# A DeltaNet recurrence that prepares its next tile early, and a merge whose pool is opened during the last attention

## The chip, the cores and the metric

The kernel runs on one core of a Trainium2 chip. Its metric is the device time of one execution in microseconds (us); smaller is better. The engines are named as the profile names them: PE does matrix products (PEld is its weight loading), DVE is the vector engine, ACT the scalar engine, POOL the GpSimd engine, SP the queue that issues most of the DMAs.

## The reference, cut to what matters

One layer of a streaming encoder for 1024 prompt rows and 64 sample rows. Four branches read one projection of the normalised input; their outputs are gated and summed, and a feed-forward block follows.

```python
def token_mixers(u, past, p, l):
    proj = u @ p['w_in'][l]
    fox, dif, sb, gdn, gates = jnp.split(proj, SPLITS, axis=-1)
    o_fox  = query_sweep(fox_core, ...)      # forgetting attention
    o_diff = query_sweep(diff_core, ...)     # two softmaxes a head: p1 - lam * p2
    o_sb   = query_sweep(sb_core, ...)       # stick-breaking attention
    o_g, s_new = gated_delta_chunked(gq, gk, gv, g, beta, s0, 64)
    gate = jax.nn.sigmoid(gates).reshape(B, T, 4, D_MODEL)
    merged = sum(gate[:, :, i] * (o.reshape(B, T, 256) @ wb[i]) for i, o in enumerate(branches))
    return merged @ p['w_out'][l], new_state

def gated_delta_chunked(q, k, v, g, beta, s0, chunk):
    # free of the state: sol = triangular_solve(m + I, [v*beta, k*beta*exp(gcum)]); u0, kcum = split(sol); qk
    def step(S, xs):                         # one after the other, 64 rows each
        v_new = u_i - kc_i @ S
        o = (q_i * exp(g_i)) @ S + a_i @ v_new
        S = S * exp(g_last) + (k_i * exp(g_last - g_i)).T @ v_new
        return S, o
```

The inputs keep these shapes; the feed-forward block, the norms and the short convolution are not touched by the change.

## The kernel before, in words

The work is cut into row tiles of 128 (tile 8 is the 64 sample rows). A tile framework records the instructions, gives each tile of memory a slot from its pool, orders the instructions of each engine ahead of time and writes the semaphores; on the chip each engine then takes its own list from the front. A pool's tag has a fixed number of slots (`bufs`). Products are done in float16 pairs, so most of them are three matmuls (high x high, high x low, low x high).

Stages in order of time: the projections and the DeltaNet's first pass; then three attentions, `attend_sb`, `attend_fox` and `attend_diff`, each over 2 head pairs and 9 query tiles; then the merge; then the output projection and the feed-forward block. Two lists of generators are worked off beside the attentions. `dense` holds PE-heavy work; from `attend_sb` on its main part is `spill_gates`: 16 units of 256 gate columns (4 a branch, in the order sb, fox, diff, gdn), each of 6 pieces, each piece 24 matmuls into one PSUM bank `pgs`, an ACT eviction `ths` and a POOL DMA to DRAM `gtd_sb`, `gtd_fox`, `gtd_diff`, `gtd_gdn`. `side` holds latency-bound work: during `attend_diff` it is `gdn_seq`, the recurrence. `fill(us)` is called once for each query tile (twice in `attend_diff`); it takes that much from `dense` and one step from `side`.

A gate unit's weights come through the tag `w32` of the pool `wp`: two DMA loads of 128x1024 into two of its **three** slots, each split into a float16 pair by ACT (`wh`) and DVE (`wl`, L64), after which the slot is free. The merge's branch weights use the same tag, under the name `wb32`, and are split into `wbh` and `wbl`.

`gdn_seq` opens the pool `gp3` on the right side of SBUF. For each of nine tiles it loads, makes the state-free part (`py`, `px`, the block-diagonal `ttbd`, `pu`, `pk`, `kc`), then takes one or two steps of 64 rows, each a chain `pks`, `vn`, `vh`, `pds`, `S32`, `Sh`/`Sl`. Its PSUM tiles come from the tag `g`, two banks. The result goes through `osg` to `od_gdn`.

Only when `attend_diff` and `gdn_seq` are recorded is `gp3` closed and the merge's pool `br` opened, also on the right side: it holds `oT` (a branch's output, read back from DRAM), `wbh`, `wbl`, and the first gate tiles `thg`. The merge takes the branches in the order sb, fox, diff, gdn, 24 pieces each: 6 matmuls into `ptb`, the gate's tanh on ACT, and DVE or POOL adds into `mg`.

In profile rows and rows of order the numbers at the ends of names are often left out or cut: `w` and `wb` are `w32` and `wb32`, `tt` and `t` are `tt32` and `t11`, `y` is `y21`, `u` is the normalised input for `pgs`, `rec1b` and `rec2b` are the records that the first pass left in DRAM.

Of the kernel before, what the change touches and what calls it, by code (L numbers as in the profile page):

```python
# [9 lines left out]
F16 = mybir.dt.float16  # L10
# [7 lines left out]
P = 128  # L18
D = 1024
# [34 lines left out]
def tile_hybrid_encoder(ctx, tc, i, o):  # L54
# [836 lines left out]

    def new_state(S32, Sh, Sl):
        acopy(Sh, S32, 16.0)
        stt(Sl, S32, 16.0, Sh, ALU.mult, ALU.subtract)

    def gdn_seq(g3):
# [20 lines left out]
        def fresh_state():  # L917
            return (g3.tile([P, NH, 64], F16, tag="Sh", name="Sh", bufs=2),
                    g3.tile([P, NH, 64], F16, tag="Sl", name="Sl", bufs=2))
# [4 lines left out]
        for hf in range(2):  # L924
            sync.dma_start(S32s[64 * hf:64 * hf + 64], i["state_gdn"][0, 0].rearrange("h d e -> d h e"))

        for t in [8] + list(range(8)):
            n = rows(t)
            nch = 1 if t == 8 else 2
            S32 = S32s if t == 8 else S32p  # L930
            if t in (8, 0):
                Sh, Sl = fresh_state()
                new_state(S32, Sh, Sl)
            t32 = t32s[t % 2]
            t11 = g3.tile([P, NH, 32], F32, tag="t11", name="t11", bufs=2)
            y21 = g3.tile([P, NH, 32], F32, tag="y21", name="y21", bufs=2)
# [2 lines left out]
            for c in range(nch):  # L939
                up, dn = slice(64 * c, 64 * c + 32), slice(64 * c + 32, 64 * c + 64)  # L940
                sync.dma_start(t32[up, :, 0:32], xv[2 * t + c, 0])
                sync.dma_start(t32[dn, :, 32:64], xv[2 * t + c, 1])
                sync.dma_start(t32[up, :, 32:64], nd[2 * t + c, :, 2].rearrange("h j i -> j h i"))
                sync.dma_start(t11[64 * c:64 * c + 32], xtv[2 * t + c])

            py = pgd("py")
            px = pgd("px")
            for c in range(nch):
                lo_, up_ = slice(64 * c, 64 * c + 32), slice(64 * c + 32, 64 * c + 64)
                for h in range(NH):  # L950
# [6 lines left out]
            for c in range(nch):  # L957
                sl = slice(64 * c, 64 * c + 64)
                acopy(bd[sl, 0, :, sl], t32[sl])
                tt(bd[sl, 1, :, sl], t32[sl], bd[sl, 0, :, sl], ALU.subtract)  # L960
            rec1 = g3.tile([P, 1536], F16, tag="rec1", name="rec1b", bufs=1)
            rec2 = g3.tile([P, 1536], F16, tag="rec2", name="rec2b", bufs=2)
            sync.dma_start(rec1[:n], r1d[t, 0:n])
            sync.dma_start(rec2[:n], r2d[t, 0:n])
            if n < P:
                vec.memset(rec2[n:], 0.0)
            qe = g3.tile([P, NH, P], F16, tag="qe", name="qe", bufs=2)
            sync.dma_start_transpose(out=qe[:, :, 0:n], in_=qed[t * P:t * P + n])
            kbe = rec1[:, 0:1024].rearrange("p (l h d) -> p l h d", l=2, h=NH)
            vb = rec1[:, 1024:].rearrange("p (l h e) -> p l h e", l=2, h=NH)  # L970
            kd = rec2[:, 0:1024].rearrange("p (l h d) -> p l h d", l=2, h=NH)
# [12 lines left out]
            pk4 = pk.rearrange("p (h i) -> p h i", h=NH)  # L984
            acopy(kc[:, :, :n], pk4[:, :, :n])
            tt(kc[64:128, :, :n], pk4[64:128, :, :n], kc[64:128, :, :n], ALU.subtract)

            zt = g3.tile([P, BW], F32, tag="zt", name="ztg", bufs=2)
            gps.dma_start(zt[:n], zd[t * P:t * P + n])
            z4g = zt.rearrange("p (h e) -> p h e", h=NH)  # L990

            po = pgd("pog")
            for c in range(nch):
                sl = slice(64 * c, 64 * c + 64)
                e4 = eg[:, c, t * NH:(t + 1) * NH]
                pks = pgd("pks")
                for h in range(NH):
                    pe.matmul(pks[sl, h * 64:h * 64 + 64], lhsT=kc[:, h, sl], rhs=Sh[:, h], start=True, stop=False)
                    pe.matmul(pks[sl, h * 64:h * 64 + 64], lhsT=kc[:, h, sl], rhs=Sl[:, h], start=False, stop=True)
                S1 = g3.tile([P, NH, 64], F32, tag="S1", name="S1", bufs=2)  # L1000
                tt(S1, S32, bc(e4[:, :, None], [P, NH, 64]), ALU.mult)
                vn = g3.tile([P, NH, 64], F32, tag="vn", name="vn", bufs=2)
                vh = vhs[c]
                stt(vn[sl].rearrange("p h e -> p (h e)"), pks[sl, 0:256], -(2.0 ** -5),
                    u0[sl].rearrange("p h e -> p (h e)"), ALU.mult, ALU.add)
                acopy(vh[sl, 0], vn[sl])
                tt(vh[sl, 1], vn[sl], vh[sl, 0], ALU.subtract)
                pds = pgd("pds")
                for h in range(NH):
                    for q, (a, b) in enumerate(((0, 0), (0, 1), (1, 0))):  # L1010
                        pe.matmul(pds[:, h * 64:h * 64 + 64], lhsT=kd[:, a, h], rhs=vh[:, b, h], start=(q == 0), stop=(q == 2))
                for h in range(NH):
                    dst = po[sl, h * 64:h * 64 + 64]
                    pe.matmul(dst, lhsT=qe[:, h, sl], rhs=Sh[:, h], start=True, stop=False)
                    pe.matmul(dst, lhsT=qe[:, h, sl], rhs=Sl[:, h], start=False, stop=False)
                    pe.matmul(dst, lhsT=aa[:, 0, h], rhs=vh[:, 0, h], start=False, stop=False)
                    pe.matmul(dst, lhsT=aa[:, 0, h], rhs=vh[:, 1, h], start=False, stop=False)
                    pe.matmul(dst, lhsT=aa[:, 1, h], rhs=vh[:, 0, h], start=False, stop=True)
                stt(S32.rearrange("p h e -> p (h e)"), pds[:, 0:256], 2.0 ** -9, S1.rearrange("p h e -> p (h e)"), ALU.mult, ALU.add)
                Sh, Sl = fresh_state()  # L1020
                if not (t == 8 or (t == 7 and c == 1)):
                    new_state(S32, Sh, Sl)
                yield 0.0
            if t == 8:
                gps.dma_start(o["s_gdn_state"][0, 0].rearrange("h d e -> d h e"), S32[0:64])
# [49 lines left out]
    with tc.issue_after(last_tanh[0].ins):  # L1075
        pre = act.preload_act_table_set("natural_log_exp_and_others")
    wide[0] = False
    with tc.issue_after(pre.ins):
        dense += [spill_gates(b, sp, d2) for b in gtd for d2 in range(4)]
        attend_sb()  # L1080
    drain(dense, proj[1])
    drain(dense, dense[0])
# [6 lines left out]
    drain(side)  # L1089
    cb_.close()  # L1090
    pj_.close()
    gd_ = ExitStack()
    g3 = gd_.enter_context(tc.tile_pool(name="gp3", bufs=1, side="right", reuse_waits="tile"))
    side.append(gdn_seq(g3))
    attend_diff()
    drain(side)
    gd_.close()
    br_ = ExitStack()
    brp = br_.enter_context(tc.tile_pool(name="br", bufs=1, side="right", reuse_waits="tile"))
    drain(dense)  # L1100
    ap_.close()
    gp_ = ExitStack()
# [12 lines left out]

    gt_pool = gp_.enter_context(tc.tile_pool(name="gates", bufs=1, reuse_waits="tile"))

    wbr = i["w_branch"][0]
    pbk = (psc, pgd, psc, pgd, psc)
    nb_ = [0]  # L1120
    mg = [(brp if d < 3 else gt_pool).tile([P, T], F32, tag=f"mg{d}", name=f"mg{d}") for d in range(KD)]
    order = ("sb", "fox", "diff", "gdn")
    for bi, b in enumerate(order):
        j = bidx[b]
        oT = brp.tile([P, 2, 2, T], F16, tag="oT", name="oT", bufs=2)
        if b in ("sb", "fox"):
            for pr in range(2):
                gps.dma_start(oT[:, :, pr], od[b][pr])
        else:
            sync.dma_start_transpose(out=oT.rearrange("p l r t -> p (l r) t"), in_=od[b])  # L1130
        wbh = brp.tile([P, 2, D], F16, tag="wbh", name="wbh", bufs=2)
        wbl = brp.tile([P, 2, D], F16, tag="wbl", name="wbl", bufs=2)
        for k in range(2):
            w32 = wp.tile([P, 4, BW], F32, tag="w32", name="wb32", bufs=3)
            wv = w32.rearrange("p a b -> p (a b)")[:, :D]
            sync.dma_start(wv, wbr[j, k * P:(k + 1) * P])
            acopy(wbh[:, k], wv, WS)
            stt(wbl[:, k], wv, WS, wbh[:, k], ALU.mult, ALU.subtract)
        last = bi == len(order) - 1
        for c in {1: (1, 2), 2: (3, 0)}.get(bi, ()):  # L1140
            load_out(c)
        for d, (off, n) in [(d, PIECES[p]) for p in (0, 2, 1) for d in range(KD)] if last else \
                [(d, p) for d in range(KD) for p in PIECES]:
            th = (brp if bi == 0 else gt_pool).tile([P, 364], F32, tag=("th0" if bi == 0 else "th"), name="thg",
                                                    bufs=(4 if bi == 0 else 12))
            sync.dma_start(th[:, :n], gtd[b][d * P:(d + 1) * P, off:off + n])
            act.activation(th[:, :n], th[:, :n], AF.Tanh)
            pt = pbk[nb_[0] % len(pbk)]("ptb")
            nb_[0] += 1
            last_ptb = gemm_a(pt, (wbh, wbl), d * P, oT[:, 0], oT[:, 1], off, n, 2)  # L1150
            if bi == 0:
                stt(mg[d][:, off:off + n], th[:, :n], 1.0, pt[:, :n], ALU.add, ALU.mult)
            else:
                stt(th[:, :n], th[:, :n], 1.0, pt[:, :n], ALU.add, ALU.mult)
                tt(mg[d][:, off:off + n], mg[d][:, off:off + n], th[:, :n], ALU.add,
                   eng=vec if (d % 3 == 2 if last else off >= 728) else gps)
            if last:
                sl = slice(off, off + n)
                acopy(mT[:, 0, d, sl], mg[d][:, sl], 0.5 * IWS)
                stt(mT[:, 1, d, sl], mg[d][:, sl], 0.5 * IWS, mT[:, 0, d, sl], ALU.mult, ALU.subtract)  # L1160
# [351 lines left out]
```

## Time and profile before

| | |
|---|---|
| time, median of 3 runs | 1853.46 us (1852.04 to 1858.17) |
| the profiled execution | 1856.4 us, of which the span of the trace is 1854.7 us |
| PE busy | 1740.3 us, 94% of the span, 14364 matmuls |
| DVE busy | 1251.0 us, 67% |
| ACT busy | 866.6 us, 47% |
| POOL busy | 307.1 us, 17% |

The busy share is a mean over stages with different limits, and a matmul's length is modelled, so the table says only where to look. Places in time are given in us from the start of the span.

### The profile page before, as it was taken

The page shows a single profiled execution, that of the slowest core. Times are in us where ns is not written, and L with a number is a line of the kernel's source. Part 1 is how long each engine was busy: PE and PEld are TensorE (multiplying, and loading weights), DVE is VectorE, ACT ScalarE, POOL GpSimd, SP SyncE. Part 2 cuts the span into 40 slices and gives each one's busy share as a digit, 9 for nine tenths or more (in the row PEclk, how much of TensorE's full clock was granted, in tenths as well). Part 3 has the DMA queues.
Part 4 walks back from the last instruction along what each step waited for, and adds up shares of the span by engine and source line. Part 5 has one row for each costly group of instructions (what it writes and reads, how often), then busy time and mean ns, then how long its engine had stood idle before and what let it go on. Part 6 is the DMA issues. An engine that isn't in the chain of part 4 may idle for free.

```text
span 1854.7 us, 36819 instructions
## 1 busy us (share of the span) xinstructions
PE 1740.3 (94%) x14364; PEld 1236.0 (67%) x14364; DVE 1251.0 (67%) x2589; ACT 866.6 (47%) x1819; POOL 307.1 (17%) x478
## 2 busy tenths in 40 slices
PE   7999898999999899999758999999999999999998
PEld 5678775655776566666534578777758668577573
DVE  7659872877788567877847886757637456465465
ACT  6336553998666345655544533423314223133132
POOL 2104342121110212332313630000000000000002
PEclk9999999999999999999759999999999999999999
DMA  7287689888899875755548746412211113012113
GB/s 226 49 100 205 207 241 229 181 156 183 186 242 213 180 177 126 172 143 142 118 152 282 223 138 106 102 52 69 69 35 58 46 46 92 25 45 69 35 47 102
DMA packets 412767, 244.29 MB, mean 132 GB/s; under 512 B 266278, under 2 KB 390450, under 8 KB 412456
## 3 DMA queue, kind: packets, MB, share of 16 engines
q1 hardware_dynamic: 398944, 205.67, 46.0%
q0 software_dynamic: 13648, 36.27, 6.7%
q8 instruction: 112, 1.84, 0.4%
q14 instruction: 63, 0.52, 0.1%
HBM read 123.39 MB, written 60.53 MB: 99 GB/s over the span
## 4 chain that ended last, share of the span: by engine, by line
PE 58%; DVE 6%; DMA 6%; ACT 2%; issue 1%; POOL 0%; SPq 0%; DVEq 0%; POOLq 0%; ACTq 0%
PE po L1434 12%; PE pgs L183 4%; PE pgs L185 4%; PE pgs L184 4%; DMA pt<-st 3%; PE pb L1317 3%; PE pb L1318 3%; PE pb L1319 3%; PE pa L1319 2%; PE pc L1318 2%; PE pa L1318 2%; PE pa L1317 2%; PE pc L1319 2%; PE pc L1317 2%; PE pout L165 1%
## 5 line engine op out<-in xcount | busy, mean ns | idle before, releaser
L183 PE MATMUL pgs<-u,wh 128*128 128x364 f16 (+1 forms) x768 | 246.2, 321 | 6.0 <-ACT ths L61 5.9
L185 PE MATMUL pgs<-u,wl 128*128 128x364 f16 (+1 forms) x768 | 246.2, 321 | 0.0
L184 PE MATMUL pgs<-u,wh 128*128 128x364 f16 (+1 forms) x768 | 246.1, 320 | 0.0
L1434 PE MATMUL po<-wh,hT 128*128 128x512 f16 (+1 forms) x792 | 238.2, 380 | 0.6 <-DVE x2a L64 0.6
L1434 PEld LDWEIGHTS <-hT 128*128 128x128 f16 (+1 forms) x1188 | 109.2, 99 | 120.0 <-issue 7.6
L64 DVE SCALAR_TENSOR_TENSOR x2a<-po,x2a 128x512 f32<-128x512 f32 x108 | 74.4, 689 | 141.5 <-PE po L1434 141.3
L61 ACT ACTIVATE wh<-w32f 128x1024 f16<-128x1024 f32 (+1 forms) x90 | 80.3, 926 | 160.7 <-PE po L1434 111.6
L1317 PE MATMUL pb<-X,wh 128*128 128x288 f16 (+1 forms) x528 | 147.5, 280 | 2.4 <-DMA X<-nsh 2.1
L64 DVE SCALAR_TENSOR_TENSOR wl<-w32f,wh 128x1024 f16<-128x1024 f32 (+1 forms) x90 | 94.6, 1065 | 80.0 <-ACT wh L61 79.9
L1318 PE MATMUL pb<-X,wh 128*128 128x288 f16 (+1 forms) x528 | 147.8, 280 | 0.0
L1319 PE MATMUL pb<-X,wl 128*128 128x256 f16 (+1 forms) x528 | 146.9, 280 | 0.0
L1434 PE MATMUL po<-wl,hT 128*128 128x512 f16 (+1 forms) x396 | 142.1, 379 | 0.0
L1317 PEld LDWEIGHTS <-wh 128*128 128x128 f16 x1232 | 120.8, 98 | 31.3 <-issue 2.3
L1318 PEld LDWEIGHTS <-wh 128*128 128x128 f16 x1232 | 120.8, 98 | 30.4 <-issue 2.4
L1319 PEld LDWEIGHTS <-wl 128*128 128x128 f16 x1232 | 120.8, 98 | 27.0 <-issue 0.4
L184 PEld LDWEIGHTS <-wh 128*128 128x128 f16 x912 | 89.8, 98 | 56.6 <-issue 8.5
L165 PE MATMUL pd<-wh,u 128*128 128x256 f16 (+1 forms) x448 | 123.8, 276 | 1.3 <-ACT e L61 1.3
L183 PEld LDWEIGHTS <-wh 128*128 128x128 f16 x912 | 89.9, 99 | 52.3 <-issue 2.7
L167 PE MATMUL pd<-wh,u 128*128 128x256 f16 (+1 forms) x448 | 123.7, 276 | 0.0
L185 PEld LDWEIGHTS <-wl 128*128 128x128 f16 x912 | 89.9, 99 | 50.6 <-issue 1.4
L166 PE MATMUL pd<-wl,u 128*128 128x256 f16 (+1 forms) x448 | 123.5, 276 | 0.0
L71 POOL TENSOR_SCALAR fss<-fss 128x1 f32<-128x1 f32 (+1 forms) x9 | 2.0, 219 | 661.6 <-ACT fsq L1463 661.6
(393 smaller groups left out, 4662.6 us busy)
## 6 DMA issues: line engine op xcount, KB each, us to landing
w<-in_w_in_dram SPq DMA_DIRECT2D x56, 512.0 KB, 5.3
w32f<-in_w_ffn_gate_dram SPq DMA_DIRECT2D x20, 512.0 KB, 5.0
w32f<-in_w_ffn_up_dram SPq DMA_DIRECT2D x20, 512.0 KB, 3.9
w32f<-in_w_ffn_down_dram SPq DMA_DIRECT2D x20, 512.0 KB, 3.8
xt<-in_x_prompt_dram SPq DMA_DIRECT2D x8, 512.0 KB, 6.6
wb<-in_w_branch_dram SPq DMA_DIRECT2D x8, 512.0 KB, 5.8
w<-in_w_out_dram SPq DMA_DIRECT2D x8, 512.0 KB, 3.7
x2a<-in_x_prompt_dram SPq DMA_DIRECT2D x8, 512.0 KB, 7.2
```

The source lines that it names most:

```text
L61: return act.activation(out, in_, AF.Copy, scale=scale)
L64: return vec.scalar_tensor_tensor(out=out, in0=in0, scalar=s, in1=in1, op0=op0, op1=op1)
L165: pe.matmul(ps[:n, :N], lhsT=a, rhs=wh[:, k, :N], start=(k == 0), stop=False)
L166: pe.matmul(ps[:n, :N], lhsT=a, rhs=wl[:, k, :N], start=False, stop=False)
L167: pe.matmul(ps[:n, :N], lhsT=b, rhs=wh[:, k, :N], start=False, stop=(k == K - 1))
L183: pe.matmul(ps[:, :n], lhsT=a, rhs=xh[:, k, off:off + n], start=(k == 0), stop=False)
L184: pe.matmul(ps[:, :n], lhsT=a, rhs=xl[:, k, off:off + n], start=False, stop=False)
L185: mm = pe.matmul(ps[:, :n], lhsT=b, rhs=xh[:, k, off:off + n], start=False, stop=(k == K - 1))
L1317: pe.matmul(ps[:, :n], lhsT=wh[:, k], rhs=xh_, start=(start and k == 0), stop=False, skip_group_check=not start)
L1318: pe.matmul(ps[:, :n], lhsT=wh[:, k], rhs=xl_, start=False, stop=False, skip_group_check=not start)
L1319: mm = pe.matmul(ps[:, :n], lhsT=wl[:, k], rhs=xh_, start=False, stop=(k == 3), skip_group_check=not start)
L1434: pe.matmul(ps[h * n:h * n + n], lhsT=hts[k + h][:, a, tk:tk + n], rhs=w[:, k + h], start=(k == 0 and a == 0 and w is wh), stop=(k + nh >= ...
```

## The change

Three edits. In `gdn_seq` the tile's work is cut into `load` and `prepare`; the next tile's `load` stands ahead of a tile's steps and its `prepare` between the two steps. `px` becomes a part of `py`'s bank and `pks` a part of `po`'s, so that a two-step tile takes 6 banks in turn where it took 9. In the main sequence 16 us of gate units are taken ahead of `attend_sb`, and the gate generators no longer stand under the order edge of the table load. And a generator `open_merge` follows `gdn_seq` on `side`: it closes `gp3`, opens `br`, and records the loads of the branches sb and fox, so that these are recorded while `attend_diff` is still being recorded.

```diff
-        for t in [8] + list(range(8)):
+        def load(t):
...
+            sync.dma_start(rec1[:n], r1d[t, 0:n])
+            sync.dma_start(rec2[:n], r2d[t, 0:n])
...
+        def prepare(t, n, nch, t11, y21, rec1, rec2, qe, zt):
...
             py = pgd("py")
-            px = pgd("px")
+            px = py[:, 128:256]
...
+        order = [8] + list(range(8))
+        here = prepare(*load(order[0]))
+        for k, t in enumerate(order):
+            after = load(order[k + 1]) if k + 1 < len(order) else None
+            _, n, nch, u0, kc, kd, aa, qe, zt = here
...
             po = pgd("pog")
+            pks = po[:, 256:512]
             for c in range(nch):
...
-                pks = pgd("pks")
...
+                if c == 0 and after is not None:
+                    here = prepare(*after)
                 yield 0.0
...
+    dense += [spill_gates(b, sp, d2) for b in gtd for d2 in range(4)]
+    fill(16.0)
     with tc.issue_after(pre.ins):
-        dense += [spill_gates(b, sp, d2) for b in gtd for d2 in range(4)]
         attend_sb()
...
+    def load_branch(b):
+
+        brp, j = brps[0], bidx[b]
         oT = brp.tile([P, 2, 2, T], F16, tag="oT", name="oT", bufs=2)
...
         for k in range(2):
             w32 = wp.tile([P, 4, BW], F32, tag="w32", name="wb32", bufs=3)
             wv = w32.rearrange("p a b -> p (a b)")[:, :D]
-            sync.dma_start(wv, wbr[j, k * P:(k + 1) * P])
+            sync.dma_start(wv, i["w_branch"][0][j, k * P:(k + 1) * P])
             acopy(wbh[:, k], wv, WS)
             stt(wbl[:, k], wv, WS, wbh[:, k], ALU.mult, ALU.subtract)
+        branch[b] = oT, wbh, wbl
+
+    def open_merge():
+        gd_.close()
+        brps.append(br_.enter_context(tc.tile_pool(name="br", bufs=1, side="right", reuse_waits="tile")))
+        load_branch("sb")
+        yield 0.0
+        load_branch("fox")
+        yield 0.0
+
+    side += [gdn_seq(g3), open_merge()]
+    attend_diff()
+    drain(side)
```

The order of the instructions before and after shows where this lands. First SP's list during the first head pair of `attend_diff`. `w_...<-in_w_in` are gate weights, `pt` and `qt` the attention's transposes, `rec1b`, `rec2b` and `qe` DeltaNet loads. In the kernel before:

```order
L963 DMA rec1b<-r1d 128x1536
L491 DMA_TRANSPOSE qt<-qd_diff 128x4x128
L447 DMA_TRANSPOSE pt<-st 128x14x128
L149 DMA w_12195<-in_w_in_dram 128x4x256
L149 DMA w_12547<-in_w_in_dram 128x4x256
L968 DMA_TRANSPOSE qe<-qed 128x4x128
L447 DMA_TRANSPOSE pt<-st 128x12x128
L964 DMA rec2b<-r2d 128x1536
```

In the changed kernel, at the same place (row 384 of SP's list in both for the first of the two loads):

```order
L943 DMA rec1b<-r1d 128x1536
L447 DMA_TRANSPOSE pt<-st 128x14x128
L1123 DMA wb_11963<-in_w_branch_dram 128x1024
L1123 DMA wb_12085<-in_w_branch_dram 128x1024
L447 DMA_TRANSPOSE pt<-st 128x12x128
L491 DMA_TRANSPOSE qt<-qd_diff 128x4x128
```

A third such load, `wb_11959`, stands 12 rows earlier, where the kernel before has the gate load `w_12191`; so three branch loads in a row take the places of three gate loads.

Next, the place in SP's list of the changed kernel where gate weights come again: behind the last transposes of `attend_diff` (`pt` 128x2x128 is its last query tile) and behind the first gate tiles of the merge (`thg`).

```order
L447 DMA_TRANSPOSE pt<-st 128x4x128 x2
L447 DMA_TRANSPOSE pt<-st 128x2x128 x2
L1173 DMA thg<-gtd_sb 128x364 x2
L1173 DMA thg<-gtd_sb 128x360
L1173 DMA thg<-gtd_sb 128x364
L1173 DMA thg<-gtd_fox 128x364 x2
L1123 DMA wb_12089<-in_w_branch_dram 128x1024
L1173 DMA thg<-gtd_fox 128x360
L149 DMA w_12195<-in_w_in_dram 128x4x256
```

Between these two places SP's list of the changed kernel has no `in_w_in` load; that of the kernel before has seven more behind `w_12547` before it comes to its own first branch load.

Last, PE's list of the changed kernel: the end of its eleventh gate unit (matmuls into `pgs`), and what follows it.

```order
L184 MATMUL pgs<-u_103,wh 128x360
L185 LDWEIGHTS wl
L185 MATMUL pgs<-u_103,wl 128x360
L980 LDWEIGHTS ttbd_8731
L980 MATMUL pu<-rec1b,ttbd_8731 128x64
L980 LDWEIGHTS ttbd_8731
L980 MATMUL pu<-rec1b,ttbd_8731 128x64
L983 LDWEIGHTS rec1b
L983 MATMUL pk<-ttbd_8731,rec1b 128x128
L604 LDWEIGHTS pt
```

The next `pgs` matmul comes some 2000 rows on, behind the whole attention, the whole recurrence and the merge's first 9 pieces (`ptb`):

```order
L185 LDWEIGHTS wbl
L185 MATMUL ptb<-oT,wbl 128x360
L183 LDWEIGHTS wh
L183 MATMUL pgs<-u_103,wh 128x364
L184 LDWEIGHTS wh
L184 MATMUL pgs<-u_103,wh 128x364
```

Ahead of the gap stand 1584 of the 2304 gate matmuls, behind it 720 (30 pieces), and these stand between the merge's pieces of the branch sb: the first 9 of its 24 ahead of them, 9 among them, 6 behind. In the kernel before the 720 stand between the attention's and the recurrence's matmuls, and all `ptb` behind them. In both lists the 1584th gate matmul lies at the same place of the attention: 894 and about 896 score matmuls stand ahead of it.

## Rows read from the trace of the kernel before

**Rows 1.** The page: busy time, and PE and its granted clock in 40 slices.

```profile
PE 1740.3 (94%) x14364; PEld 1236.0 (67%) x14364; DVE 1251.0 (67%) x2589; ACT 866.6 (47%) x1819; POOL 307.1 (17%) x478
...
PE   7999898999999899999758999999999999999998
...
PEclk9999999999999999999759999999999999999999
```

**Rows 2.** Stretches, us: busy of each engine (count), PE's granted clock, DMA share, GB/s.

```profile
752.00:903.00 151.00, 150.98 (x1443) 100.22 (x1441) 121.02 (x400) 89.15 (x248) 42.14 (x74) 1.00 0.64 150
903.00:925.00 22.00, 12.24 (x150) 9.20 (x146) 17.87 (x77) 11.34 (x43) 9.53 (x17) 0.62 0.34 81
903.00:950.00 47.00, 28.46 (x365) 22.77 (x362) 30.52 (x109) 23.07 (x70) 12.10 (x21) 0.56 0.35 100
950.00:961.00 11.00, 0.29 (x6) 0.26 (x4) 5.19 (x7) 4.04 (x6) 5.37 (x8) 0.50 0.28 91
961.00:1000.00 39.00, 28.24 (x150) 16.10 (x150) 18.51 (x28) 18.28 (x29) 0.00 (x0) 0.89 0.84 286
1000.00:1083.00 83.00, 75.62 (x536) 48.55 (x536) 76.11 (x125) 44.60 (x92) 56.75 (x53) 0.98 0.76 225
```

**Rows 3.** The gate pieces' stores (L1055): count, ns min/median/max, first and last start.

```profile
L1055 POOL DMA_DIRECT2D gtd_sb<-ths x24: 540/557/1044, 290.7 to 414.3; - x24
L1055 POOL DMA_DIRECT2D gtd_fox<-ths x24: 540/557/633, 416.9 to 658.8; - x24
L1055 POOL DMA_DIRECT2D gtd_diff<-ths x17: 539/542/614, 662.8 to 744.5; - x17
L1055 POOL DMA_DIRECT2D gtd_diff<-ths x7: 539/556/614, 752.2 to 783.7; - x7
L1055 POOL DMA_DIRECT2D gtd_gdn<-ths x24: 539/556/625, 787.5 to 902.5; - x24
```

**Rows 4.** Timeline, PE: gate matmuls one behind the other (start, us).

```profile
664.10 0.32 PE L183 MATMUL pgs<-u,wh 128*128 128x364 f16 x1
664.26 0.32 PE L184 MATMUL pgs<-u,wh 128*128 128x364 f16 x1
664.41 0.32 PE L185 MATMUL pgs<-u,wl 128*128 128x364 f16 x1
664.57 0.32 PE L183 MATMUL pgs<-u,wh 128*128 128x364 f16 x1
```

**Rows 5.** Groups of DVE from 752 to 903: busy, mean ns, idle before.

```profile
L646 DVE TENSOR_REDUCE sm<-psc 128x1 f32<-128x512 f32 (+4 forms) x57 | 29.7, 537 | 3.0 <-PE psc L458 2.1 <-PE psc L456 0.2
...
L64 DVE SCALAR_TENSOR_TENSOR wl<-w,wh 128x1024 f16<-128x1024 f32 x7 | 8.4, 1215 | 0.4 <-ACT wh L61 0.4
```

**Rows 6.** Timeline, DVE: `kc` of two tiles in turn, near the recurrence's end.

```profile
924.42 0.69 DVE L67 TENSOR_TENSOR kc<-pk,kc 64x512 f16<-64x512 f32 x1 [1.28 <-ACT kc L61]
941.40 0.69 DVE L67 TENSOR_TENSOR kc<-pk,kc 64x512 f16<-64x512 f32 x1 [2.10 <-ACT kc L61]
```

**Rows 7.** Timeline, POOL and PE: from the recurrence's last matmul to the merge's first.

```profile
950.05 0.24 PE L1018 MATMUL pog<-vh,rec2b 128*64 128x64 f16 x1
...
956.37 0.62 POOL L1040 DMA_DIRECT2D od_gdn<-osg  x1 [2.20 <-DVE osg L67]
957.18 1.47 POOL L1128 DMA_DIRECT2D oT<-od_sb  x2 [0.20 <-issue]
...
961.30 0.46 PE L183 MATMUL ptb<-oT,wbh 128*128 128x364 f16 x1 [11.01 <-DMA oT<-od_sb]
961.55 0.51 PE L184 MATMUL ptb<-oT,wbh 128*128 128x364 f16 x1
961.86 0.51 PE L185 MATMUL ptb<-oT,wbl 128*128 128x364 f16 x1
```

**Rows 8.** Groups of DVE in the merge, 957 to 1083.

```profile
L64 DVE SCALAR_TENSOR_TENSOR thg<-thg,ptb 128x364 f32<-128x364 f32 (+1 forms) x72 | 35.4, 521 | 2.8 <-PE ptb L185 1.6 <-ACT thg L1147 0.8 <-POOL mg L67 0.4
...
L64 DVE SCALAR_TENSOR_TENSOR wl<-w,wh 128x1024 f16<-128x1024 f32 x6 | 7.3, 1222 | 6.8 <-ACT wh L61 6.8
```

**Rows 9.** Timeline, PE: the two waits in 300 to 312, ahead of the first attention.

```profile
302.33 0.46 PE L183 MATMUL pgs<-u,wh 128*128 128x364 f16 x1 [3.91 <-ACT ths L61]
310.52 0.31 PE L183 MATMUL pgs<-u,wh 128*128 128x360 f16 x1 [1.69 <-ACT ths L61]
```

More of the change, by code (lines that the diff above doesn't have):

```diff
@@ L925, in gdn_seq @@
             sync.dma_start(S32s[64 * hf:64 * hf + 64], i["state_gdn"][0, 0].rearrange("h d e -> d h e"))
-        for t in [8] + list(range(8)):
+        def load(t):
             n = rows(t)
             nch = 1 if t == 8 else 2
[L930 to L933, printed above, removed]
             t32 = t32s[t % 2]
@@ L944, in gdn_seq @@
                 sync.dma_start(t11[64 * c:64 * c + 32], xtv[2 * t + c])
+            rec1 = g3.tile([P, 1536], F16, tag="rec1", name="rec1b", bufs=1)
+            rec2 = g3.tile([P, 1536], F16, tag="rec2", name="rec2b", bufs=2)
+            sync.dma_start(rec1[:n], r1d[t, 0:n])
+            sync.dma_start(rec2[:n], r2d[t, 0:n])
+            if n < P:
+                vec.memset(rec2[n:], 0.0)
+            qe = g3.tile([P, NH, P], F16, tag="qe", name="qe", bufs=2)
+            sync.dma_start_transpose(out=qe[:, :, 0:n], in_=qed[t * P:t * P + n])
+            zt = g3.tile([P, BW], F32, tag="zt", name="ztg", bufs=2)
+            gps.dma_start(zt[:n], zd[t * P:t * P + n])
+            return t, n, nch, t11, y21, rec1, rec2, qe, zt
+        def prepare(t, n, nch, t11, y21, rec1, rec2, qe, zt):
+            t32 = t32s[t % 2]
             py = pgd("py")
-            px = pgd("px")
+            px = py[:, 128:256]
             for c in range(nch):
@@ L960, in gdn_seq @@
                 tt(bd[sl, 1, :, sl], t32[sl], bd[sl, 0, :, sl], ALU.subtract)
[L961 to L968, printed above, removed]
             kbe = rec1[:, 0:1024].rearrange("p (l h d) -> p l h d", l=2, h=NH)
@@ L986, in gdn_seq @@
             tt(kc[64:128, :, :n], pk4[64:128, :, :n], kc[64:128, :, :n], ALU.subtract)
-            zt = g3.tile([P, BW], F32, tag="zt", name="ztg", bufs=2)
-            gps.dma_start(zt[:n], zd[t * P:t * P + n])
+            return t, n, nch, u0, kc, kd, aa, qe, zt
+        order = [8] + list(range(8))
[3 more added lines that the diff above has]
+            _, n, nch, u0, kc, kd, aa, qe, zt = here
             z4g = zt.rearrange("p (h e) -> p h e", h=NH)
+            S32 = S32s if t == 8 else S32p
+            if t in (8, 0):
+                Sh, Sl = fresh_state()
+                new_state(S32, Sh, Sl)
             po = pgd("pog")
+            pks = po[:, 256:512]
             for c in range(nch):
@@ L1091, in tile_hybrid_encoder @@
     pj_.close()
-    gd_ = ExitStack()
+    gd_, br_ = ExitStack(), ExitStack()
     g3 = gd_.enter_context(tc.tile_pool(name="gp3", bufs=1, side="right", reuse_waits="tile"))
-    side.append(gdn_seq(g3))
+    brps, branch = [], {}
+    def load_branch(b):
+        brp, j = brps[0], bidx[b]
+        oT = brp.tile([P, 2, 2, T], F16, tag="oT", name="oT", bufs=2)
+        if b in ("sb", "fox"):
+            for pr in range(2):
+                gps.dma_start(oT[:, :, pr], od[b][pr])
+        else:
+            sync.dma_start_transpose(out=oT.rearrange("p l r t -> p (l r) t"), in_=od[b])
+        wbh = brp.tile([P, 2, D], F16, tag="wbh", name="wbh", bufs=2)
+        wbl = brp.tile([P, 2, D], F16, tag="wbl", name="wbl", bufs=2)
+        for k in range(2):
+            w32 = wp.tile([P, 4, BW], F32, tag="w32", name="wb32", bufs=3)
+            wv = w32.rearrange("p a b -> p (a b)")[:, :D]
+            sync.dma_start(wv, i["w_branch"][0][j, k * P:(k + 1) * P])
+            acopy(wbh[:, k], wv, WS)
+            stt(wbl[:, k], wv, WS, wbh[:, k], ALU.mult, ALU.subtract)
+        branch[b] = oT, wbh, wbl
[7 more added lines that the diff above has]
+    side += [gdn_seq(g3), open_merge()]
     attend_diff()
     drain(side)
-    gd_.close()
-    br_ = ExitStack()
-    brp = br_.enter_context(tc.tile_pool(name="br", bufs=1, side="right", reuse_waits="tile"))
+    brp = brps[0]
     drain(dense)
@@ L1116, in tile_hybrid_encoder @@
     gt_pool = gp_.enter_context(tc.tile_pool(name="gates", bufs=1, reuse_waits="tile"))
-    wbr = i["w_branch"][0]
     pbk = (psc, pgd, psc, pgd, psc)
@@ L1123, in tile_hybrid_encoder @@
     for bi, b in enumerate(order):
[L1124 to L1135, printed above, removed]
-            sync.dma_start(wv, wbr[j, k * P:(k + 1) * P])
-            acopy(wbh[:, k], wv, WS)
-            stt(wbl[:, k], wv, WS, wbh[:, k], ALU.mult, ALU.subtract)
+        if b not in branch:
+            load_branch(b)
+        oT, wbh, wbl = branch[b]
         last = bi == len(order) - 1
```

## The prediction

> **What bounds the kernel now.** I read the page first. PE is busy for 94% of the span [rows 1], and of the 40 slices (46.4 us each) the only two with a lowered clock are the 20th and 21st, 881 to 974 us. So there is one soft place, around the end of the last attention, and the change is built around it. I then cut this place into stretches [rows 2]. The reader is to see three regimes:
>
> - 752 to 903: PE is busy all the time at the full clock, since gate pieces fill every gap. DVE is at 121.0 of 151 us, 80%. PE sets the pace.
> - 903 to 950: the gates are used up (the last store is at 902.5 [rows 3]); the rest of the attention and the recurrence run alone, PE at 28.5 of 47 us and a granted clock of 0.56.
> - 950 to 961 PE waits, then comes the merge, to 1083: with holes to 1000 (28.2 of 39 us busy), then bound by DVE (76.1 of 83 us, 92%).
>
> In the 97 us from 903 to 1000 PE does 28.5 x 0.56 + 0.3 x 0.5 + 28.2 x 0.89 = 41 us of work in terms of the full clock [rows 2]. Some 56 us can be had there at most.
>
> **What the order does with the change.** The gain needs the gate pieces to last to the end of the attention. The lists in the section on the change say otherwise. `gdn_seq` gives a step at every `fill` and is recorded out after 18 of the 36 of `attend_diff`; `open_merge` follows at once, and so is recorded ahead of the twelfth gate unit (the numbers in the names rise with the recording: `wb_11959` to `wb_12089`, then `w_12195`). Loads of `w32` are issued far ahead, as slots come free, in that order. Three of the four branch loads thus take all three slots in place of gate loads. They can't give them back: their `wbh` and `wbl` live in `br`, which lies where `gp3` lies and can be had only when the recurrence has ended on the chip. The next gate load stands behind the attention's last transposes, and PE's list has no gate matmul from the 1584th until the merge's tenth piece. 1584 matmuls are 66 pieces; sb and fox make 48, so it is the 18th of diff, which is stored at 752.2 [rows 3]. From there the attention and the recurrence run without filler, and 30 gate pieces come later. An engine takes its list from the front, so no speed of another engine mends this.
>
> [...]
>
> **The sum**, against the profiled execution, from 752 to the merge's end at 1083:
>
> 1. The stretch without gates, D. Before, the same work ended with the recurrence's last matmul at 950.05 [rows 7], 198 us after 752. Its DVE work is 121.0 + 30.5 us [rows 2], less the 7 gate splits of 1.215 us [rows 5], so 143 us. Its PE work is smaller: 720 gate matmuls at 0.154 us from start to start [rows 4] are 111 of the 151 us, the other 40 take 80 at half the clock (0.50 was granted in 950 to 961), and with the 28.5 after 903 that is 109. So D lies between 143 (DVE never waits) and 198 (nothing gets faster). The nearest row without gates is 903 to 925, where DVE was busy 17.9 of 22 us, 81%; that would make 177. ACT no longer evicts gates there and PE's queue is short, so I take the middle of the ends, 170. The attention ends at 922, 28 us earlier than before.
> 2. The gap to the merge stays. The `oT` loads still stand behind the last `od_gdn` store on POOL's queue, and the same chain took 11.0 us [rows 7]. That `oT` is recorded earlier gains nothing, since its pool opens no earlier relative to the recurrence's end. 933.
> 3. The 30 gate pieces and the 18 sb pieces that stand ahead of them or among them: (720 + 18 x 6) x 0.154 = 127 us, PE-bound at the full clock. The first pieces run at 0.303 us a matmul [rows 7], as before; for 20 matmuls that is 3 us more. 1063.
> 4. The rest of the merge, 78 pieces. Before, 150 matmuls or 25 pieces were done by 1000 and the other 71 took 83 us with DVE at 92% [rows 2]. Now 7 more pieces (7 x 0.52 us [rows 8]) and four more weight splits at 1.22 us come in there, 8.5 us of DVE work or 9 us at that share: 92. 1155.
> 5. The 16 us of gates ahead of `attend_sb`: they can fill only what PE idles there, 3.9 and 1.7 us [rows 9]. Bounds 0 and 6; I take 3. 1152.
>
> So the merge ends at 1152 where it ended at 1083: +69. Behind it nothing is moved.
>
> The other parts cost about nothing here. The number of instructions on each engine is the same within two rows. The recurrence, which had 17.0 us a tile when it ran alone [rows 6], now makes the next tile's state-free part between the two steps; that shortens it only where nothing else holds it, and in D DVE's 143 us hold it. If DVE did not, the six tiles left at 752 would take 6 x 17 = 102 us even serially, less than D. Fewer PSUM banks a tile is worth at most the waits on `g`, which are inside D's bounds. The earlier loads put a tile's DMAs (4 or 8 small ones, `rec1`, `rec2`, `qe` on SP, `zt` on POOL) ahead on in-order queues; behind a `rec1` that waits for its single buffer stand the attention's `pt` and `qt`. No row shows such a wait; at the least it is nothing, and at the most it pushes D toward its upper end.
>
> The profiled 1856.4 plus 69 is 1925; the median of three runs lay 2.9 below the profiled execution, so 1922. I round to **1920 us**.
>
> **The rivals.**
>
> *DVE saturates.* Without PE in the way DVE runs nearly without waiting, D = 148. For it: in 752 to 903 its largest group waited only 3.0 us in 57 operations [rows 5]. Against: 81% where no gate stood in the way [rows 2]. Time: 1920 - 22 = 1898; with all small terms at their good ends (D 143, step 4 at 83, no clock term, 6 for step 5) the merge ends at 752 + 143 + 11 + 127 + 83 - 6 = 1110, so +27, 1881.
> [...]
>
> *The pace stays.* The three PSUM banks of the scores and the clock at half hold D at 198, and the transition costs 10 us more, because `oT`, 19 gate tiles and the first gate weights come in one burst. For it: PE would be busy 109 of 198 us at half the clock, as in 903 to 950 (61%). Time: 1920 + 28 + 10 = 1958.
>
> *The change does what it sets out to do* (the other sign). Gates last to the end of the attention, the recurrence is hidden, and of the 56 us only the 11 us gap remains: 1853 - 45 = 1808. It decides at one place: whether a gate load is issued between 752 and the recurrence's end. For break-even D would have to be 170 - 69 = 101, less than DVE's 143 us of work in it. The lists speak against it, and nothing in the trace for it.
>
> *Nothing to be seen.* The pieces displaced are made up exactly by the filled holes; it needs the same D near 101.
>
> **How the numbers follow.** The forecast (D 155 to 185) has 0.55, the saturated DVE 0.20, the pace of before 0.20, the other sign 0.03, nothing 0.02. The range reaches into the two neighbours: 1888 to 1952 leaves out half of the pace rival above (one in ten), and below the lowest part of the first rival and the last two cases (another one in ten). A change of 0.3%, 5.6 us, is about what three runs (spread 0.3%) can tell from none. Faster 0.03, same 0.02, slower 0.95.
>
> **What would show it.** In the changed profile: no store to `gtd_gdn` before the last `od_gdn` store, then all 24; PE's granted clock near 0.5 over some 150 us from about 750 with PE under 70% busy; the three `wb` loads landed near 750 and their first `wbh` some 170 us later; the merge's start about 25 us earlier than 961, and its end 60 to 80 us later than 1083. The prediction is wrong if gate matmuls run in that stretch, if D is under 140, or if the merge's DVE-bound part shrinks by more than the 9 us that I add to it.

## The result, and the profile after

The changed kernel took 1925.1 us (median of four runs, 1918.1 to 1936.3); the kernel before, run beside it, 1855.8 (1852.0 to 1868.3). The ratio is 1.037, with a 95% interval from 1.030 to 1.044. The forecast of 1920 us and its range of 1888 to 1952 hold. The profiled execution has a span of 1921.5 us.

The page of the changed kernel, PE and its granted clock in 40 slices of 48 us:

```profile
PE 1767.0 (92%) x14364; PEld 1252.4 (65%) x14364; DVE 1249.0 (65%) x2589; ACT 868.2 (45%) x1819; POOL 310.3 (16%) x478
...
PE   7999898989977998766799889999999999999998
...
PEclk9999999999989999566899999999999999999999
```

Where [rows 1] have two slices with a lowered clock there are now five: the 17th to the 20th (769 to 961 us), and the 12th (528 to 576 us), which lies in `attend_fox`. Every engine runs as many instructions as before. Of the 67 us by which the span is longer, PE is busy for 27 (1767.0 against 1740.3), with the same matmuls at a lowered clock for longer (the 208 `psc` matmuls of L456 have a median of 379 ns against 327); in the other 40 it stands.

The gate pieces' stores, by tensor: the eighteenth of `gtd_diff` ends the first group, and the second group holds the rest (the store at 759.8 is in both).

```profile
L1067 POOL DMA_DIRECT2D gtd_diff<-ths x18: 539/557/633, 671.3 to 759.8; - x18
L1067 POOL DMA_DIRECT2D gtd_diff<-ths x7: 542/542/587, 759.8 to 963.5; - x7
L1067 POOL DMA_DIRECT2D gtd_gdn<-ths x24: 540/542/543, 965.5 to 1058.2; - x24
```

The branch weights, SP's loads and ACT's splits on the timeline:

```profile
672.11 0.40 SPq L1123 DMA_DIRECT2D wb<-in_w_branch_dram  x1
696.69 2.40 SPq L1123 DMA_DIRECT2D wb<-in_w_branch_dram  x2
919.53 2.93 ACT L61 ACTIVATE wbh<-wb 128x1024 f16<-128x1024 f32 x3
925.54 0.38 SPq L149 DMA_DIRECT2D w<-in_w_in_dram  x1
```

Three loads go out by 699 us and are read first at 919.5, behind the recurrence's last matmul at 914.6. For that time they hold the three `w32` slots: the next gate load on SP's queue goes out at 925.5. The next gate store after 759.8 comes at 944.3; in [rows 3] 30 of them follow on the one at 752.2 by 902.5.

The stretches, in the columns of [rows 2]: ahead of the last gate piece, without gates, the gap, the gates with the branch sb, the rest of the merge.

```profile
752.00:759.00 7.00, 6.86 (x61) 4.46 (x59) 6.49 (x21) 3.85 (x10) 2.10 (x4) 1.00 0.70 108
759.00:914.60 155.60, 102.00 (x1104) 74.35 (x1105) 136.94 (x500) 88.00 (x270) 36.92 (x62) 0.60 0.47 100
914.60:925.30 10.70, 0.56 (x9) 0.38 (x7) 7.08 (x15) 6.53 (x11) 8.36 (x13) 0.50 0.38 119
925.30:1061.00 135.70, 134.91 (x861) 84.74 (x861) 28.80 (x37) 43.12 (x78) 16.30 (x30) 0.98 0.48 161
1061.00:1150.00 89.00, 77.00 (x537) 48.53 (x536) 80.55 (x125) 47.29 (x92) 58.96 (x53) 0.98 0.75 218
```

The reader is to see two stretches of opposite kinds side by side. In 759 to 914.6 PE is busy for 66% at a granted clock of 0.60, and DVE for 88%; in 925 to 1061 PE is busy all the time at full clock, and DVE for 21%. Before, the two kinds of work lay on top of each other.

What PE waits for in the stretch without gates:

```profile
PE po L604 <- DMA pt<-st: 15.7, 11, 3.6
PE psc L456 <- ACT p L655: 10.9, 18, 1.8
PE pog L1009 <- DVE Sl L64: 5.1, 5, 2.2
PE pog L1024 <- DVE vn L64: 4.4, 5, 1.4
```

These are many short waits for transposes, for the softmax's PSUM banks and for the recurrence's chain: the holes that the gates had covered.

### The profile page after: what moved, and what is told of

Its sections match the earlier page's. It is cut to its first block, busy times and chain, and to the rows that moved or that the text cites. A ratio compares the mean times of both kernels' runs of the same rounds, so it can differ in the third digit from the quotient of the medians.

```text
span 1921.5 us, 36810 instructions
## 1 busy us (share of the span) xinstructions
PE 1767.0 (92%) x14364; PEld 1252.4 (65%) x14364; DVE 1249.0 (65%) x2589; ACT 868.2 (45%) x1819; POOL 310.3 (16%) x478
## 4 chain that ended last, share of the span: by engine, by line
PE 53%; DVE 8%; DMA 7%; issue 2%; ACT 1%; POOL 1%; SPq 0%; DVEq 0%; POOLq 0%; ACTq 0%
PE po L1461 12%; DMA pt<-st 4%; PE pgs L185 4%; PE pgs L183 3%; PE pgs L184 3%; PE pb L1345 3%; PE pb L1344 3%; PE pb L1346 3%; PE pc L1345 2%; PE pc L1346 2%; PE pa L1346 2%; PE pc L1344 2%; PE pa L1345 2%; PE pa L1344 2%; PE pout L165 1%
## 5 line engine op out<-in xcount | busy, mean ns | idle before, releaser
L64 DVE SCALAR_TENSOR_TENSOR wl<-w,wh 128x1024 f16<-128x1024 f32 x62 | 74.8, 1229 | 108.8 <-ACT wh L61 80.3
L165 PE MATMUL pd<-wh,u 128*128 128x256 f16 (+1 forms) x448 | 123.8, 276 | 1.5 <-ACT e L61 1.5
```

The lines of the kernel that those rows point to most:

```text
L64: return vec.scalar_tensor_tensor(out=out, in0=in0, scalar=s, in1=in1, op0=op0, op1=op1)
L165: pe.matmul(ps[:n, :N], lhsT=a, rhs=wh[:, k, :N], start=(k == 0), stop=False)
```

## The experiments

In their expectations "slots", "recurrence" and "pool" are the three theories: the branch weights hold the `w32` slots; the new order in `gdn_seq` costs the time; the pool opened early blocks a queue by itself. Times of one kernel's runs differ by 1% and more (29 runs of the kernel before, beside only_gdn: 1849.8 to 1875.6 us), so ratios to the kernel before, run beside each, are compared.

### The three edits one by one

**only_open**: `gdn_seq` and the start of `attend_sb` as before, only the early pool with its loads.

```diff
-    side.append(gdn_seq(g3))
-    attend_diff()
-    drain(side)
-    gd_.close()
...
+    side += [gdn_seq(g3), open_merge()]
+    attend_diff()
+    drain(side)
```

> The early pool alone, in the kernel before: open_merge on the list beside the attention, the recurrence and the gate start as they were. Slots theory (branch weights hold the three w32 slots until the recurrence ends): about as slow as the changed kernel, 1915 to 1940 us, no gate store between about 760 us and the end of the recurrence. Recurrence theory (the new order inside gdn_seq costs the time): within 0.5% of before, 1847 to 1865. Pool theory (the pool and its oT loads, recorded early, block POOL's queue, whatever the slots): also 1915 or more, so this run parts the recurrence theory from the other two.

Ratio 1.038 (1.033 to 1.043). The early pool with its loads gives the whole loss by itself; the recurrence theory falls.

**late_open**: the changed kernel with the pool opened where it was.

```diff
-    side += [gdn_seq(g3), open_merge()]
+    side.append(gdn_seq(g3))
     attend_diff()
     drain(side)
+    gd_.close()
+    brps.append(br_.enter_context(tc.tile_pool(name="br", bufs=1, side="right", reuse_waits="tile")))
```

> The changed kernel with br opened where it was before, behind attend_diff and gdn_seq; the new recurrence and the early gates stay. Slots and pool theories: gates fill again to about 900 us, the time is that of before or a little under it, 1835 to 1860; the recurrence has 98 us after 903 of which it may win a few. Recurrence theory: 1900 or more.

0.999 (0.997 to 1.002). The loss is gone, and nothing is won.

**only_gdn**: late_open with the gates' start as before, so that only the recurrence is new.

> The new gdn_seq alone, in the kernel before (pool at its old place, gates not ahead of attend_sb). The kernel with the late pool showed no difference from before, but its profile had the stretch from the last gate store to the last od_gdn store at 39 us where before has 54, and the last od_fox store 337 to 341 us behind the first score matmul where before has 327. Theory of two parts: the recurrence wins some 10 us in the tail, the early gates lose as many in attend_fox; then this run gives 0.990 to 0.996 of before. Rival: the recurrence's edit does nothing by itself: 0.997 to 1.003.

0.996 (0.993 to 1.000): a gain of some 7 us, at the edge of what this can tell. The traces show why it is so small. The recurrence's last matmul comes 14 us behind the last score matmul (950.7 - 936.6), in the kernel before 40 (950.1 - 909.7), and over all kernels run 11 to 25 with the new recurrence, 32 to 58 with the old; but the last score comes 287 us behind the last `od_fox` store (936.6 - 650.0), before 268 (909.7 - 641.3). Of the 26 us won in the recurrence's tail the attention gives back 18.

**only_fill**: the kernel before with the gates taken ahead of `attend_sb`.

```diff
+    dense += [spill_gates(b, sp, d2) for b in gtd for d2 in range(4)]
+    fill(16.0)
     with tc.issue_after(pre.ins):
-        dense += [spill_gates(b, sp, d2) for b in gtd for d2 in range(4)]
         attend_sb()
```

> The 16 us of gates ahead of attend_sb alone, in the kernel before. Theory of two parts: attend_fox has less filler and shows its waits for transposes, the last od_fox store comes 337 to 341 us behind the first score, 1.002 to 1.006 of before. Rival: no effect, 327 us there and 0.998 to 1.002; the forecast gave this part a gain of 0 to 6 us, 0.997 to 1.000.

1.007 (1.004 to 1.010), a loss of some 12 us. The last `od_fox` store comes at 660.6 us, 336.7 behind the first score matmul at 323.9; before it was 641.3 - 314.0 = 327.3. The two parts are of opposite sign and cancel in late_open. The gain of the recurrence shows once more there: late_open is only_fill with the new recurrence, and the two intervals (0.997 to 1.002 and 1.004 to 1.010) don't meet.

### What the early pool takes

**late_weights**: the changed kernel with pool and `oT` early, but the branch weights loaded at their branch's turn in the merge.

```diff
+    def load_weights(b):
+        j = bidx[b]
+        _, wbh, wbl = branch[b]
...
     for bi, b in enumerate(order):
         if b not in branch:
             load_branch(b)
+        load_weights(b)
         oT, wbh, wbl = branch[b]
```

> The changed kernel with br opened early and oT loaded early, but the branch weights loaded where they were. Slots theory: 1835 to 1860, as with the late pool. Pool theory: 1900 or more. Recurrence theory: 1900 or more.

0.9995 (0.996 to 1.003). The pool and the early `oT` loads cost nothing; the pool theory falls, and the weights are the cause.

**own_slots**: the changed kernel whole, but the early weights in space of `br` that is not yet used.

```diff
-            w32 = wp.tile([P, 4, BW], F32, tag="w32", name="wb32", bufs=3)
-            wv = w32.rearrange("p a b -> p (a b)")[:, :D]
+            if b in ("sb", "fox"):
+                t_ = (2 * (b == "fox") + k) % 3
+                w32 = brp.tile([P, T], F32, tag=f"mg{t_}", name="wb32")
+            else:
+                w32 = wp.tile([P, 4, BW], F32, tag="w32", name="wb32", bufs=3).rearrange("p a b -> p (a b)")
+            wv = w32[:, :D]
```

> The changed kernel whole, with the branch weights of sb and fox loaded into the space of mg0 to mg2 in br, so that they take no w32 slot. Slots theory: 1835 to 1860; the loads now wait for br and come after the recurrence, so that little is won on the late pool, within 5 us of it. Pool theory: 1900 or more, since the loads wait in SP's queue for the pool. Recurrence theory: 1900 or more.

0.999 (0.996 to 1.002). So it is not that the loads are recorded early, but which slots they take.

**sb_only**: the changed kernel with two branch loads early instead of four.

```diff
     def open_merge():
         gd_.close()
         brps.append(br_.enter_context(tc.tile_pool(name="br", bufs=1, side="right", reuse_waits="tile")))
         load_branch("sb")
         yield 0.0
-        load_branch("fox")
-        yield 0.0
```

> The changed kernel with open_merge cut to the branch sb: two branch loads are recorded ahead of the gate units instead of four. Slots theory: two of the three w32 slots are held and one is left, the gate loads go on one at a time through it, so the gates run on through the attention: 1845 to 1875 us. If any held slot, or the pool, stops the gates: 1900 or more.

0.998 (0.994 to 1.002). The branch weights of sb are held from 674 and 699 us to 956 here too, and the gate loads go on through the one slot that is left. SP's timeline, gate loads between the second `wb` load and the third:

```profile
698.79 0.36 SPq L1123 DMA_DIRECT2D wb<-in_w_branch_dram  x1
700.86 0.38 SPq L149 DMA_DIRECT2D w<-in_w_in_dram  x1
732.06 0.38 SPq L149 DMA_DIRECT2D w<-in_w_in_dram  x1
738.80 0.39 SPq L149 DMA_DIRECT2D w<-in_w_in_dram  x1
...
857.38 0.39 SPq L149 DMA_DIRECT2D w<-in_w_in_dram  x1
864.52 0.33 SPq L1123 DMA_DIRECT2D wb<-in_w_branch_dram  x1
```

Ten loads where the changed kernel has none, and PE is busy for 151.0 of the 151 us from 752 to 903. One slot of three is enough; the whole loss hangs on the third.

### Late gates without held slots

**defer**: the kernel before, with the loads of the last five gate units queued on SP behind the `rec2` load of the last recurrence tile.

```diff
-            sync.dma_start(rec2[:n], r2d[t, 0:n])
+            marks[t] = sync.dma_start(rec2[:n], r2d[t, 0:n])
...
     drain(side)
+    for g, t in zip(gu[11:], (7, 7, 7, 7, 7)):
+        ahead.append(marks[t].ins)
+        drain([g])
+        ahead.clear()
```

> The kernel before, with the loads of its last five gate units queued on SP behind the load of rec2 for the last recurrence tile; no pool is opened early and no branch weight takes a slot of the attention. If late gates alone carry the price, whatever makes them late: the attention runs without filler, ends earlier and the 30 pieces come behind it, 1905 to 1935 us, as in the changed kernel; a little less if the gates start in the recurrence's last 20 us. If it is the held slots or the early pool that cost in some other way: within 1% of before.

1.016 (1.009 to 1.022): a loss, by the medians less than half of that of the changed kernel, and with 1890 us below the 1905 that was expected. The windows show why: without gates until 866.6, then gates beside the recurrence's end and the gap, then gates and the merge's first pieces.

```profile
745.00:875.00 130.00, 87.94 (x843) 60.90 (x844) 115.69 (x401) 75.17 (x221) 29.37 (x45) 0.55 0.55 123
875.00:955.00 80.00, 80.00 (x715) 52.76 (x714) 35.22 (x106) 37.23 (x93) 25.42 (x43) 1.00 0.52 163
955.00:1003.00 48.00, 47.92 (x313) 30.30 (x312) 11.64 (x15) 16.22 (x28) 6.51 (x12) 1.00 0.48 163
```

The same 30 pieces are late, but they come back at 866.6 us, ahead of the recurrence's end, and fill its last part and the gap to the merge. In the changed kernel they can't, since the slots wait for `br`. So lateness is one part of the price, and being locked out until the recurrence has ended the other. By the medians 29 of some 67 us come with defer, but its interval reaches from 18 to 41 us, so which part is the larger isn't shown.

### Why the early gates cost

**fill_debt**: only_fill, with the account of `fill` set back ahead of `attend_fox`. The account (`debt`) is what `fill` was asked for less what it took; while it is below zero the next call takes less.

```diff
     dense.insert(0, proj[2])
+    debt[0] = -0.1592
     side.append(gdn_solve())
     attend_fox()
```

> only_fill, with the account that fill keeps (debt) set back at the start of attend_fox to the value that it has there in the kernel before, -0.16 us; the early gates had left it at -2.66. With that PE's list from attend_fox on is that of before: 144 more projection matmuls stand ahead of the 144th score row group instead of 72. Pacing theory (the early gates cost time because the account, and with it the filler of attend_fox, is shifted): the last od_fox store is again 327 to 331 us behind the first score, 0.998 to 1.002 of before. Rival (the gates taken ahead of attend_sb cost by themselves, in the first attention or ahead of it): 1.004 to 1.009, as only_fill.

(The counts in it are mixed up. In the traces 1728 projection matmuls into `pd` have run ahead of the 190th matmul into `psc`, counted from the first score, in the kernel before and in fill_debt, 1656 in only_fill. The 72 that differ took 9 us in the kernel before, 513.9 to 522.8.) 0.998 (0.994 to 1.002), and the last `od_fox` store comes 655.5 - 330.5 = 325.0 us behind the first score. What PE waits for from 475 to 665 us, only_fill:

```profile
PE pv L468 <- DMA pt<-st: 15.7, 9, 3.0
PE psc L456 <- DMA qt<-qd_diff: 4.0, 1, 4.0
```

and fill_debt:

```profile
PE pv L468 <- DMA pt<-st: 10.6, 8, 2.4
PE pv L468 <- DVE os L64: 2.7, 2, 2.1
```

and the kernel before:

```profile
PE pv L468 <- DMA pt<-st: 8.9, 8, 2.7
PE pv L468 <- DVE os L64: 5.8, 1, 5.8
```

The early gates cost nothing where they stand. They leave the account 2.5 us lower, and a projection unit of `attend_fox` comes later by it. From the last `od_sb` store to the last `od_fox` store PE then stands for 20 us (only_fill), against 15 in the kernel before and 13 in fill_debt; most of the difference to fill_debt is waits for transposes, while against the kernel before it is less clear which waits grow. All traces agree on the stretch: from the first score to the last `od_fox` store it takes 337 to 341 us in the six kernels with early gates, and 324 to 331 in the seven without them and in fill_debt.

### The search for a version that beats both

**own_nofill**: own_slots without the gates ahead of `attend_sb`.

> The changed kernel with the branch weights of sb and fox in the space of mg0 to mg2 (own_slots) and without the gates ahead of attend_sb. If the parts add up: the new recurrence alone gave 0.996 of before, the early gates 1.007, and in own_slots the merge took 106 us from its first to its last ptb where before took 114; so 0.989 to 0.995, 1840 to 1852 us beside a before of 1862. Rival: the shorter merge and the shorter recurrence win the same time, and the sum is no more than that of the recurrence alone, 0.995 to 0.999.

0.997 (0.994 to 1.001). The merge takes 1066.6 - 958.6 = 108 us from first to last `ptb` (before 114), but the wait ahead of it has grown to 16.7 us (before 11.0, [rows 7]); by the median the parts don't add up, as the rival had it, though the interval still reaches the upper part of what adding up would give (0.989 to 0.995).

**own_spread** and **own_last2**: own_nofill with the loads of the last four, or two, gate units queued as in defer.

```diff
+    for g, t in zip(gu[12:], (4, 5, 6, 7)):
```

> own_nofill, with the loads of the last four gate units queued on SP behind the rec2 loads of the recurrence tiles 4, 5, 6 and 7, so that in PE's list 720 gate matmuls are spread evenly to the end of the attention's scores, where own_nofill has them used up some 30 us before. Theory (the soft place after the last gate is lack of filler): the full clock lasts to the last score, of the 39 to 50 us from the last gate store to the last od_gdn store 15 to 30 go, 0.975 to 0.987 of before. Rival (the recurrence's chain and DVE set the end of this stretch, filler or not): the same as own_nofill within 0.3%.

> own_nofill, with only the last two gate units held, behind the rec2 loads of tiles 6 and 7: the gates stop for some 20 score groups and come back at the end, the last of them beside the recurrence's last two tiles. Filler theory: the tail is filled as in own_spread or better, but a soft place opens ahead of it; between own_nofill and own_spread, 0.980 to 0.992 of before. Rival: as own_nofill.

1.001 (0.998 to 1.003) and 0.999 (0.996 to 1.002): the filler theory fails. In own_spread the gates do last longer:

```profile
750.00:932.00 182.00, 171.66 (x1688) 111.96 (x1686) 144.47 (x472) 104.01 (x288) 48.23 (x83) 0.98 0.63 151
932.00:960.00 28.00, 15.86 (x179) 12.07 (x177) 19.75 (x71) 14.19 (x42) 11.28 (x19) 0.68 0.58 167
```

But from the first score to the last it takes 937.3 - 321.9 = 615.4 us, in own_nofill 926.5 - 309.5 = 617.0: gates taken out of the attention's busy part don't make the attention end earlier, and PE now idles there by 10 us. Why it takes as long with less PE work wasn't taken apart further.

## Why the prediction was right, and where its terms were not

The mechanism holds step by step: `wb` loads take the slots, no gate matmul runs in the stretch, and 30 pieces come behind it. That PE takes its list from the front is seen there: from 759 to 914.6 it stood for 53.6 of the 155.6 us, and none of the 720 gate matmuls that stand further back in its list ran. The experiments show it from both sides: the early pool alone gives 1.038, and the change with other slots, or with one slot left, gives 0.999 and 0.998. The terms, read from the changed kernel's trace:

| term of the sum | forecast | measured |
|---|---|---|
| start of the stretch without gates (752.2 before) | 3 us earlier | 759.8, 7.6 later |
| D, to the recurrence's last matmul | 170 | 914.6 - 759.8 = 155 |
| gap to the merge | 11 | 925.3 - 914.6 = 10.7 |
| gates and 18 sb pieces | 130 | 925.3 to 1055.5, the last gate matmul: 130 |
| rest of the merge | 92 | to 1151, 1.5 us behind the first `pout` matmul of L165 (1149.6) as 1083 was (1081.5): 95.5 |
| merge's end | 1152 | 1151 |

Two terms were off, by 11 us late and by 15 us early, and cancelled each other but for the 3.5 us of the merge's rest; that the sum meets the merge's end within 1 us is luck.

The early gates: "Bounds 0 and 6; I take 3" had the sign wrong. The step looked only at the idle time of PE ahead of the first attention. In the traces the same 168 gate matmuls stand ahead of the eighth score matmul with and without them, so nothing was won there, and what they moved was the account that paces the filler later. By itself that costs 12 us (only_fill). In the changed kernel's trace the last `od_fox` store comes 655.6 - 314.3 = 341 us behind the first score, 14 more than before; 7.6 of them are left where the stretch without gates starts.

D: "that shortens it only where nothing else holds it, and in D DVE's 143 us hold it" failed. With the recurrence of before, in only_open, D is 917.8 - 751.1 = 166.7 us, within 4 us of the 170; with the new one it is 155. Cut at the last score matmul, D of only_open and then D of the changed kernel:

```profile
751.10:886.20 135.10, 84.29 (x851) 59.00 (x851) 117.11 (x429) 75.06 (x232) 29.04 (x49) 0.59 0.48 102
886.20:917.80 31.60, 18.99 (x236) 15.03 (x234) 19.91 (x68) 16.83 (x47) 9.51 (x16) 0.50 0.41 115
759.80:903.50 143.70, 94.07 (x1009) 68.00 (x1010) 126.86 (x453) 81.41 (x247) 31.14 (x51) 0.61 0.47 103
903.50:914.60 11.10, 7.93 (x96) 6.35 (x96) 10.08 (x48) 5.80 (x22) 5.10 (x9) 0.50 0.31 66
```

In both DVE does 137 us of work, and while the scores run it is busy for 87 to 88%. With the recurrence of before a tail of 32 us follows in which it is at 63%; with the new one the tail is 11 us. So DVE did not hold all of D: in the tail of only_open PE is at 60% and ACT at 53%, so that no engine is near its limit there and D ends with waits of the recurrence's chain (PE's longest is 4.7 us for `vh`, DVE's 2.2 each for `pds` and `kc`), which the prepared tile shortens. (The changed kernel has the early gates as well, so the 12 us are not the recurrence's alone to the last one.) The measured 155 lies between the forecast's 170 and the 148 of the rival in which DVE saturates, nearer to the latter, and at the lower end of the 155 to 185 that the forecast had named. The 143 in which DVE never waits would have been 12 us too few: over D DVE was busy for 136.9 of 154.8 us, 88%.

Of the signs, the clock was granted at 0.60 instead of near 0.5, the `wb` loads went out at 672 to 699 us instead of near 750, so that they waited 220 to 247 us instead of 170, and the merge began 36 us earlier than before, not 25 to 28, by the shorter D; its end, 68 us later, was within 60 to 80.

"Some 56 us can be had there at most" was a bound that nothing came near: with the slots mended, the gates spread and the recurrence prepared early, the best of the kernels run, only_gdn, has 0.996, and its interval ends at 1.000.

## What to carry to other kernels

A tile that is loaded early into a shared tag holds its slot until its reader has run (the `wb` loads here for 220 to 247 us); if the reader needs a pool that opens late, the slot is gone for that long, and whoever shares the tag stands still. Count the slots: three of three taken cost 67 us here, two of three nothing. Look also at what a pacing account carries on: 16 us of work moved at one place cost 12 us a whole attention later.

Filler is worth what it covers. In the changed kernel 111 us of gate matmuls left a stretch of 198 us, and with the recurrence of before (only_open) that stretch shrank by only 198 - 167 = 31 us; run later, with PE busy all the time (925 to 1061), they took their full 111.

In the 155 us at 66% of PE the row that names the cause is a `wb` load 220 us ahead of its reader, not any of the waits in between.

## What was not expected of the hardware

The same instructions ahead of the first attention ended at times that lie up to 12 us apart. In the kernel before, only_open, only_gdn and defer nothing ahead of the first score matmul is changed, and it starts at 314.0, 308.7, 319.8 and 308.1 us. ACT's timeline shows the wait that differs: the third gate eviction needs one of two `ths` tiles back from its store to DRAM. In only_open:

```profile
295.13 0.47 ACT L61 ACTIVATE ths<-pgs 128x360 f32<-128x360 f32 x1 [6.14 <-DMA gtd_sb<-ths]
```

and in only_gdn:

```profile
309.01 0.47 ACT L61 ACTIVATE ths<-pgs 128x360 f32<-128x360 f32 x1 [20.79 <-DMA gtd_sb<-ths]
```

In these 20 us (290 to 310) the DMA engines show a share of 1.14 and 257 GB/s in only_open, 1.18 and 129 GB/s in only_gdn: as busy, at half the rate. What slows them in some executions isn't settled. 12 us are 0.6% of the time, as much as the smaller parts measured here are worth.
